# The state space of a two-layer decoder trunk: its rotation tables, its Toeplitz table and the order of its narrow products

## The chip, the core and the metric

The kernel runs on one core of a Trainium2 chip. The core has five engines with a queue each: TensorE (PE; its weight loads are shown as PEld), VectorE (DVE), ScalarE (ACT), GpSimd (POOL) and SyncE (SP, which here only issues DMAs). ACT and POOL issue DMAs too. The metric is the device time of one execution in microseconds, lower is better. All arithmetic is float32 or float32r (a float32 product whose operand is rounded; a weight is split into a high and a low part and three products make one exact one).

## What is computed

The trunk has two layers. The first is a diagonal complex state space (S5) with a gate, the second an attention layer with three branches; the change touches the first alone.

```python
u, z = split(x @ w_in, 2)                  # x: 512 x 2048, u and z: 512 x 1024
dt = exp(log_dt); mag = exp(lam_re * dt)
a = mag * exp(i * lam_im * dt)             # 64 groups x 64 states, complex
bbar = ((a - 1) / lam) * (b_re + i b_im)   # per group: 64 states x 16 channels
h[t] = a * h[t-1] + bbar @ u[t]            # per group, over 512 steps
y = real(c @ h) + d * u
g = gelu(y)
y = g * sigmoid(g @ w_glu + b_glu)
x1 = layer_norm(alpha * x + (y * silu(z)) @ w_out)
```

The kernel works the recurrence out by 64 chunks of 8 steps (`L = 8`, `NCH = 64`). Within a chunk it is a product with a Toeplitz table of the impulse response. Between chunks the states are turned by exp(-i phi chunk), which leaves a real scan. Eight tiles (`ct`) of 8 groups (`GP = 8`) are worked on one after the other.

## The kernel before

Layer 0 (`layer0_in`) multiplies x by w_in in dense products: one call of `mm3` is three products of 128x512, and 64 such calls make the first four tiles of u while x comes in, 192 more make the other twelve tiles of u and z (`L0_TILES`). Then two tiles of `g @ w_glu` follow, with two calls for each of eight k; their k-th pair needs the state space's tile k (`while s5.done < k: bg.step()`). After every call of `mm3` the scheduler `Background` is asked (`bg.tick`) to emit a stage of another chain. One such call is called a slot below. The order in which instructions are emitted is the order in which each engine works them off.

Lane 0 of the scheduler is `S5.chain`. It first runs `params` (19 stages on DVE, 4 slots apart), then the letters of `START`, then those of `CYCLE` once for each tile; a letter takes a slot. Letter t is the next stage of `tables(ct + 1)`, p of `tables(ct + 2)`, a of `apply(ct)`, r is `rotation`, and a dot is a pause. Lane 1 (`bring`) loads u of a tile back in another layout. Lane 2 holds `turns`, which `params` starts at its twelfth stage, and later `land`, which brings gelu(y) back through DRAM (`y_d`).

- `S5.__init__`, L333 to L337: POOL loads the mask `tri`; DVE zeroes a tile of tag `ta`, and POOL writes it to the front pad of the table's scratch in DRAM, `k_d`. `params` then takes the same tag `ta` for its scratch (L351), and its loads L360 to L362 (lam_re, lam_im, log_dt) wait for that write.
- `turns`, L439 to L465, on POOL: doublings of the angle, kept on the unit circle, into `AC` and `AS` (six rotations, by 8, 16, ... 256 steps). Its scratch is in tag `ta` too, so the first `tables(0)` on DVE (L513, tag `ta`) waits for its last use (L461).
- `rotation(ct)`, L467 to L491, on POOL: the tables `C` and `Sn` (128 x 8 x 64) by six doublings, 34 instructions a tile. `apply` multiplies by them at L613 (C) and L619 (Sn) and again at L629 and L631.
- `tables(ct)`, L493 to L569: DVE makes B1, B2 (L513 to L518), W1 (L528 to L533) and Q (L539, L541, L550). PE makes kps in 16 narrow instructions (L547), ACT copies it, DVE adds d, and SP writes it to `k_d` (L553). SP reads it back in one overlapping DMA as the Toeplitz table `Tz` (L558, 128 x 8 x 128), and POOL multiplies it by the mask (L560). PE transposes Q (L566), ACT copies the result to `Bst`.
- `apply(ct)`, L591 to L643, in four stages: s (L607, 16 instructions), its copy `e2` (L611), which ACT's queue sends through two DMAs that swap its halves, and L613; then L619, L620, the scan L625, another swap on SP's queue and L629; then L631 and L632 make `e1`; then the 32 instructions of yps (L636 with `Tz`, L637 with `W1` and `e1`), gelu on ACT (L640) and the DMA out.
- `SLOT`, `TPACE`, `START` and `CYCLE` are at L680 to L688.

PE runs what it is given in order, so a narrow product whose operand is late holds up the dense ones behind it.

Of the kernel before, what the change touches and what calls it, by code (L numbers as in the profile page):

```python
# [25 lines left out]
G = 64  # L26
GP = 8
L = 8
# [9 lines left out]
class Weights:  # L38
    """Streams units of 128 x <=1024 float32 from DRAM and splits each into w = h + l, both float32r."""
# [19 lines left out]
    def _split(self):  # L59
# [3 lines left out]
        if i in self.side:  # L63
            # high and low side by side, per k
# [18 lines left out]
    def ahead(self, i, loads=RAW - 1):  # L83
        """Units up to i are split, and the loads behind them are under way."""
# [13 lines left out]
class Background:  # L98
    """Stages of independent chains, put between the matrix products that they don't depend on.

    A stage yields how many products must come between it and the next of its chain, or False if it has to wait.
    """
# [55 lines left out]
def emit(tc, A, out):  # L158
# [10 lines left out]
    # the first in halves: it is waited for  # L169
# [47 lines left out]
class Core:  # L217
    """What every part uses: engines, weights, the identity."""
# [6 lines left out]
    def mm3(self, o, sh, sl, mh, ml, start, stop):  # L225
        """o (+)= s' m for s = sh + sl and m = mh + ml; what is left out, sl' ml, is below float32's rounding."""
# [10 lines left out]
def horner(V, out, x, c):  # L237
    """out = sum c[k] x**(k+1)"""
# [5 lines left out]
def exp_f32(V, x, n, r, p, ni, out):  # L244
    """out = exp(x), to float32's rounding, zero below the normal range. n, r, p, ni: scratch."""
# [16 lines left out]
def pi_parts():  # L262
    """pi cut into parts of 10 bits, so that k * part is exact for |k| < 2**14."""
# [14 lines left out]
def sincos_f32(V, th, k, r, s, t, u, sin_o, cos_o):  # L278
    """sin and cos of th: reduced by multiples of pi, Taylor series on [-pi/2, pi/2]."""
# [32 lines left out]
class S5:  # L312
    """Diagonal complex state space, by chunks of L steps.

    Rows (re | im, state) of a group; t = chunk * L + s. Within a chunk a Toeplitz product,
    between chunks a scan of the states turned by exp(-i phi chunk), which leaves it real.
    """

    def __init__(self, c, sc, gT, bg):
# [10 lines left out]
        self.AC = None  # L330
# [17 lines left out]
    def params(self):  # L348
# [61 lines left out]
        # powers of a  # L410
# [20 lines left out]
        # |a|^L  # L431
# [7 lines left out]
    def turns(self, cs, sn, c, u0, u1, u2, u3, d, e):  # L439
        """Unit rotations by 2^j theta, j = 3..8, kept on the unit circle. c, u0..3, d, e: scratch."""  # L440
        P, p1 = self.nc.gpsimd, self.p1
        AC = p1.tile([128, 6, G], F32, name="AC")
        AS = p1.tile([128, 6, G], F32, name="AS")
        c0, s0 = cs, sn
        for j in range(1, 9):
            dc, ds_ = (AC[:, j - 3], AS[:, j - 3]) if j >= 3 else ((u0, u1) if j == 1 else (u2, u3))
# [16 lines left out]
        P.tensor_scalar(AS, AS, self.sg, None, OP.mult)  # L463
        self.AC, self.AS = AC, AS
        yield 1  # L465

    def rotation(self, ct):  # L467
        P, tb = self.nc.gpsimd, self.tb
        gs = slice(ct * GP, ct * GP + GP)
        C, Sn = (tb.tile([128, GP, NCH], F32, tag=n, name=n, bufs=2) for n in ("C", "Sn"))  # L470
        t1 = tb.tile([128, GP, 32], F32, tag="rt1", name="rt1")
        t2 = tb.tile([128, GP, 32], F32, tag="rt2", name="rt2")
        P.memset(C[:, :, 0:1], 1.0)
        P.memset(Sn[:, :, 0:1], 0.0)
        for m in range(6):
            n = 1 << m
            ac = self.AC[:, m, gs].unsqueeze(2)
            as_ = self.AS[:, m, gs].unsqueeze(2)
            if n == 1:
                P.tensor_copy(C[:, :, 1:2], ac)  # L480
                P.tensor_copy(Sn[:, :, 1:2], as_)
                continue
# [1117 lines left out]
```

## Time and profile before

| | us |
|---|---|
| runs of the kernel | 1836.64, 1838.2, 1845.82 |
| median | 1838.2 |
| span of the profiled execution | 1841.3 |
| busy in it: PE, DVE, ACT, POOL | 1766.8, 1015.3, 588.4, 357.3 |

The page gives the profiled execution by its span alone; it lies between the middle and the highest of the three runs. A row of the timeline has the start, the time taken, the engine, the line, the operation, out<-in, and in brackets how long the engine had been idle before it and what released it. Matmul rows overlap (they are pipelined), so the pace is read from start to start.

### The profile page before, as it was taken

How to read it: one execution, taken by the hardware profiler on the slowest of the kernel's cores; microseconds unless marked ns; L12 is line 12 of the kernel's file. 1: busy time of each engine (PE TensorE's matmuls, PEld its weight loads, DVE VectorE, ACT ScalarE, POOL GpSimd, SP SyncE). 2: the span in 40 equal slices, each digit the busy share in tenths (PEclk: the TensorE clock that was granted, in tenths of full speed). 3: DMA queues.
4: the chain of work that ended last, by engine and by line, in shares of the span. 5: the costliest groups of instructions: out<-in, count | busy, mean ns of one | idle time of the engine just before them, and what ended most of it. 6: DMA issues, size and time to landing. Idle time of an engine off the chain costs nothing.

```text
span 1841.3 us, 22051 instructions
## 1 busy us (share of the span) xinstructions
PE 1766.8 (96%) x8455; PEld 1470.6 (80%) x8455; DVE 1015.3 (55%) x1764; ACT 588.4 (32%) x995; POOL 357.3 (19%) x500
## 2 busy tenths in 40 slices
PE   8797999999899999999999999999999999999996
PEld 6676787787778888888888888888888888888884
DVE  7775775746633355563456653555553555665336
ACT  3232232522423333332333332333332333333221
POOL 4998992002400000000000000000000000010004
PEclk9987888999999999999999999999999999999998
DMA  6443554453333322222222222222222222236332
GB/s 212 141 117 102 138 147 121 145 197 134 133 107 126 113 90 75 82 74 96 87 70 85 86 86 83 95 75 80 80 85 87 98 75 81 83 139 225 115 126 97
DMA packets 88185, 201.94 MB, mean 110 GB/s; under 512 B 24560, under 2 KB 34016, under 8 KB 87056
## 3 DMA queue, kind: packets, MB, share of 16 engines
q1 hardware_dynamic: 81392, 183.40, 29.6%
q0 software_dynamic: 3104, 10.85, 1.7%
q10 hardware_dynamic: 3584, 6.29, 1.2%
q8 instruction: 66, 1.08, 0.2%
q14 instruction: 39, 0.32, 0.1%
HBM read 176.89 MB, written 19.43 MB: 107 GB/s over the span
## 4 chain that ended last, share of the span: by engine, by line
PE 80%; POOL 9%; DVE 7%; issue 2%; DMA 2%; ACT 1%; DVEq 0%; SPq 0%; ACTq 0%; POOLq 0%
PE ps L228 23%; PE ps L230 23%; PE ps L229 22%; PE tp L1403 2%; DVE v L916 1%; POOL C L487 1%; PE s L230 1%; PE s L228 1%; PE s L229 1%; PE o L229 1%; POOL Sn L490 1%; PE o L230 1%; PE o L228 1%; POOL rt L489 1%; POOL rt L485 1%
## 5 line engine op out<-in xcount | busy, mean ns | idle before, releaser
L228 PE MATMUL ps<-x1h,hl 128*128 128x512 f32 (+1 forms) x1440 | 563.6, 391 | 1.6 <-ACT hl L77 1.6
L230 PE MATMUL ps<-x1h,hl 128*128 128x512 f32 (+1 forms) x1440 | 556.6, 387 | 0.5 <-DVE hl L79 0.5
L229 PE MATMUL ps<-x1l,hl 128*128 128x512 f32 (+1 forms) x1440 | 555.6, 386 | 0.0
L79 DVE TENSOR_TENSOR hl<-wr,hl 128x1024 fp32r<-128x1024 f32 (+1 forms) x269 | 332.1, 1238 | 319.0 <-ACT hl L77 315.3
L77 ACT CAST hl<-wr 128x1024 fp32r<-128x1024 f32 (+1 forms) x273 | 284.4, 1045 | 235.3 <-PE ps L230 206.5
L230 PEld LDWEIGHTS ps<-x1h,hl 128*128 128x128 f32 x1440 | 270.6, 188 | 57.2 <-DVE hl L79 1.0
L228 PEld LDWEIGHTS ps<-x1h,hl 128*128 128x128 f32 x1440 | 271.0, 188 | 48.2 <-ACT hl L77 1.8
L229 PEld LDWEIGHTS ps<-x1l,hl 128*128 128x128 f32 x1440 | 271.1, 188 | 46.4
L1276 POOL TENSOR_TENSOR y<-y,z 128x512 f32<-128x512 f32 x32 | 41.5, 1296 | 999.9 <-DVE z L1275 863.1
L1340 ACT ACTIVATE p<-s,m 128x384 f32<-128x384 f32 (+3 forms) x128 | 67.7, 529 | 357.5 <-DVE m L1339 357.5
L234 DVE TENSOR_TENSOR pl<-tp,ph 128x512 fp32r<-128x512 f32 (+3 forms) x128 | 62.0, 488 | 109.9 <-ACT ph L233 109.6
L228 PE MATMUL ps<-xh,hl 128*128 128x512 f32 x256 | 108.8, 425 | 6.0 <-ACT xh L751 6.0
L229 PE MATMUL ps<-xl,hl 128*128 128x512 f32 x256 | 105.3, 411 | 2.2 <-DVE xl L752 2.2
L230 PE MATMUL ps<-xh,hl 128*128 128x512 f32 x256 | 104.9, 410 | 0.8 <-DVE hl L79 0.8
L233 ACT CAST ph<-tp 128x512 fp32r<-128x512 f32 (+3 forms) x128 | 54.2, 427 | 151.3 <-PE tp L1403 151.0
L228 PE MATMUL ps<-hl,y1h 128*128 128x512 f32 x256 | 99.6, 389 | 0.0
L230 PE MATMUL ps<-hl,y1l 128*128 128x512 f32 x256 | 99.6, 389 | 0.0
L229 PE MATMUL ps<-hl,y1h 128*128 128x512 f32 x256 | 99.6, 389 | 0.0
L228 PEld LDWEIGHTS ps<-xh,hl 128*128 128x128 f32 x256 | 51.6, 202 | 17.4 <-ACT xh L751 6.0
L1339 DVE TENSOR_REDUCE m<-s 128x1 f32<-128x384 f32 (+3 forms) x128 | 62.9, 491 | 4.4
L1262 DVE SCALAR_TENSOR_TENSOR z<-z,ps 128x512 f32<-128x512 f32 x48 | 33.0, 688 | 57.1 <-ACT z L1261 57.1
L935 POOL TENSOR_TENSOR v<-v,gb 128x512 f32<-128x512 f32 x11 | 17.3, 1577 | 237.1 <-ACT v L934 237.1
(323 smaller groups left out, 2522.7 us busy)
## 6 DMA issues: line engine op xcount, KB each, us to landing
wr<-b_w_in SPq DMA_DIRECT2D x128, 512.0 KB, 3.2
wr<-kv_w SPq DMA_DIRECT2D x48, 512.0 KB, 3.2
wr<-b_w_out SPq DMA_DIRECT2D x32, 512.0 KB, 3.2
wr<-w_in_b SPq DMA_DIRECT2D x24, 512.0 KB, 3.5
wr<-w_out SPq DMA_DIRECT2D x16, 512.0 KB, 3.6
xr<-xT SPq DMA_DIRECT2D x16, 256.0 KB, 4.3
Tz<-k_d SPq DMA_DIRECT2D x8, 512.0 KB, 3.8
wr<-w_glu SPq DMA_DIRECT2D x8, 512.0 KB, 3.4
```

The lines of the kernel that those rows point to most:

```text
L77: self.nc.scalar.copy(h[:, :n], r[:, :n])
L79: eng.tensor_tensor(l[:, :n], r[:, :n], h[:, :n].bitcast(F32), OP.subtract)
L228: PE.matmul(o, sh, mh, start=start, stop=False)
L229: PE.matmul(o, sh, ml, start=False, stop=False)
L230: PE.matmul(o, sl, mh, start=False, stop=stop)
L233: self.nc.scalar.copy(h, src)
L234: self.nc.vector.tensor_tensor(l, src, h.bitcast(F32), OP.subtract)
L1262: self.nc.vector.scalar_tensor_tensor(z, z, 1.0, ps, OP.add, OP.mult)
L1276: P.tensor_tensor(y[0], y[0], z, OP.add)
L1339: self.nc.vector.tensor_reduce(m[:, b - 1, i:i + 1], s, AX.X, OP.max, negate=True)
L1340: self.nc.scalar.activation(self.p[h, b][i], s, AF.Exp, bias=m[:, b - 1, i:i + 1], accum_out=self.sums[h, b][:, i:i + 1])
L1403: PE.transpose(tp[:, 128 * (i - j):128 * (i - j) + 128], p[i][:, at:at + 128], ident)
```

## The change

- `turns` writes its six rotations into one table `R` (cos and sin, by 8, 16, 32 steps and by 64, 128, 256), with a stride of 8 elements, and then fills the other entries of two small tables of 8 with two rounds of six POOL instructions. `TPACE` is 2, not 4.
- `rotation` is six POOL instructions: products of the two small tables, broadcast along one axis each.
- `k_d` has a pad of its own for each of the 16 channels. The pad is zeroed by a memset on POOL and one DMA of 1024 runs of 448 bytes (64 before). `Tz` is read with the zeros in place, in eight DMAs, and the mask, its load and its product are gone.
- kps, s and yps are cut into 2, 2 and 4 stages, so that slots of dense products come between them. `START` has 28 letters (20 before), `CYCLE` 20 (19 before). The wait for free banks has its own letter, b, and ten pauses follow it. The rotation stands at the end of a cycle.
- gelu's output takes the buffer of `H`. The tiles of x come through seven buffers, not six.

```diff
 class S5: __init__
-        self.tri = self.p1.tile([128, L], F32, name="tri")
-        self.nc.gpsimd.dma_start(self.tri, self.A["tri"])
-        self.k_d = c.dram.tile([8, GP, PAD + 16 * 128], F32, name="k_d")
+        self.k_d = c.dram.tile([8, GP, 16, PAD + 128], F32, name="k_d")
         zero = self.tb.tile([64, PAD], F32, tag="ta", name="zero")
-        self.nc.vector.memset(zero, 0.0)
-        self.nc.gpsimd.dma_start(self.k_d[:, :, :PAD].rearrange("t g n -> (t g) n"), zero)
+        self.nc.gpsimd.memset(zero, 0.0)
+        self.nc.gpsimd.dma_start(self.k_d[:, :, :, :PAD].rearrange("t g c n -> (t g) c n"),
+                                 zero.unsqueeze(1).to_broadcast([64, 16, PAD]))
...
     def turns(self, cs, sn, c, u0, u1, u2, u3, d, e):
-        AC = p1.tile([128, 6, G], F32, name="AC")
-        AS = p1.tile([128, 6, G], F32, name="AS")
+        R = p1.tile([128, 2, 2, G, 8], F32, name="R")
+        self.R = R
+        P.memset(R[:, 0, :, :, 0], 1.0)
+        P.memset(R[:, 1, :, :, 0], 0.0)
...
+            h, at = divmod(j - 3, 3)
+            dc, ds_ = (R[:, 0, h, :, 1 << at], R[:, 1, h, :, 1 << at]) if j >= 3 else \
+                ((u0, u1) if j == 1 else (u2, u3))
...
-        P.tensor_scalar(AS, AS, self.sg, None, OP.mult)
-        self.AC, self.AS = AC, AS
+        tmp = self.tb.tile([128, 2, G, 3], F32, tag="rt1", name="rtmp")
+        for n in (2, 4):
+            sh = [128, 2, G, n - 1]
+            C, Sn = (R[:, i, :, :, 1:n] for i in range(2))
+            Co, So = (R[:, i, :, :, n + 1:2 * n] for i in range(2))
+            cn, sn_ = (R[:, i, :, :, n:n + 1].to_broadcast(sh) for i in range(2))
+            t = tmp[:, :, :, :n - 1]
+            P.tensor_tensor(Co, C, cn, OP.mult)
+            P.tensor_tensor(t, Sn, sn_, OP.mult)
+            P.tensor_tensor(Co, Co, t, OP.subtract)
+            P.tensor_tensor(So, Sn, cn, OP.mult)
+            P.tensor_tensor(t, C, sn_, OP.mult)
+            P.tensor_tensor(So, So, t, OP.add)
+            yield TPACE
+        P.tensor_scalar(R[:, 1], R[:, 1], self.sg, None, OP.mult)
+        self.turned = True
...
     def rotation(self, ct):
-        P.memset(C[:, :, 0:1], 1.0)
-        P.memset(Sn[:, :, 0:1], 0.0)
-        for m in range(6):
...
+        t = tb.tile([128, GP, NCH], F32, tag="rt1", name="rt1")
+        sh = [128, GP, 8, 8]
+        (cb, ca), (sb, sa) = ((self.R[:, i, 0, gs].unsqueeze(2).to_broadcast(sh),
+                               self.R[:, i, 1, gs].unsqueeze(3).to_broadcast(sh)) for i in range(2))
+        Cv, Sv, tv = (z.rearrange("p g (a b) -> p g a b", a=8) for z in (C, Sn, t))
+        P.tensor_tensor(Cv, ca, cb, OP.mult)
+        P.tensor_tensor(tv, sa, sb, OP.mult)
+        P.tensor_tensor(C, C, t, OP.subtract)
+        P.tensor_tensor(Sv, sa, cb, OP.mult)
+        P.tensor_tensor(tv, ca, sb, OP.mult)
+        P.tensor_tensor(Sn, Sn, t, OP.add)
...
     def tables(self, ct):
             PE.matmul(kps[:, g * 128:g * 128 + 128], B1[:, g], W1[:, g, 0:8], start=True, stop=True)
+            if g == 3:
+                yield
...
-        SP.dma_start(self.k_d[ct, :, PAD:].rearrange("g (c n) -> c g n", n=128), kp.rearrange("p g j c -> p g (j c)"))
+        SP.dma_start(self.k_d[ct, :, :, PAD:].rearrange("g c n -> c g n"), kp.rearrange("p g j c -> p g (j c)"))
         yield
         Tz = new("Tz", [GP, L, 16], 2)
-        band = self.k_d[ct, :, 0:128].rearrange("g n -> g n").unsqueeze(0)
-        SP.dma_start(Tz.rearrange("p g t c -> p g (t c)"),
-                     bass.AP(band.tensor, band.offset, [[16, 128], [PAD + 2048, GP], [1, 128]]))
-        P.tensor_tensor(Tz, Tz, self.tri.unsqueeze(1).unsqueeze(3).to_broadcast([128, GP, L, 16]), OP.mult)
+        n = PAD + 128
+        for g in range(GP):
+            band = self.k_d[ct, g, 0, 0:128].unsqueeze(0)
+            SP.dma_start(Tz[:, g].rearrange("p t c -> p (t c)"),
+                         bass.AP(band.tensor, band.offset, [[n, 16], [16, L], [1, 128]]))
...
     def apply(self, ct):
             PE.matmul(s1[:, g], t["Bst"][:, g], U[:, g], start=True, stop=True)
+            if g == 3:
+                yield
...
             PE.matmul(ys[:, g], t["W1"][:, g, 1:9].rearrange("p t c -> p (t c)"), e1[:, g], start=False, stop=True)
+            if g % 2 and g < 7:
+                yield
         self.summed = ct
-        gy = tb.tile([128, GP, NCH], F32, tag="gy", name="gy")
+        gy = tb.tile([128, GP, NCH], F32, tag="H", name="gy")
...
     def chain(self):
             elif what == "t":
-                while n == 6 and not self.banks:
+                next(t)
+            elif what == "b":
+                while not self.banks:
                     yield False
-                next(t)
-                n += 1
...
-TPACE = 4
+TPACE = 2
...
-START = 'tttttr.t.tttpp.tpr.p'
-CYCLE = 'att.ttarattp.p.pp.a'
+START = 'ttttttrb..........tttttppprp'
+CYCLE = 'aattattttatppapaaapr'
...
-    spare = ("xr", "U", "U", "e1", "e2", "H")
+    spare = ("z", "z", "U", "U", "e1", "e2", "H")
...
-            pool = st if i == 0 else s5.tb
+            pool = st if i < 2 else s5.tb
```

## Rows read from the trace of the kernel before

**Rows 1.** Stretch with the state space: busy us (instructions) by engine, clock, DMA.
```profile
71.60:333.10 261.50, 228.85 (x1135) 194.18 (x1134) 177.87 (x224) 76.52 (x110) 200.94 (x304) 0.85 0.44 125
```
**Rows 2.** Waits of PE in that stretch: us in total, times, longest us.
```profile
PE yps L636 <- POOL Tz L560: 14.8, 3, 9.6
PE kps L547 <- DVE W L533: 8.8, 1, 8.8
PE yps L637 <- DVE e L632: 5.5, 4, 2.2
```
**Rows 3.** Timeline, PE: first and last of 60 dense products, nothing between them waiting.
```profile
23.77 0.39 PE L228 MATMUL ps<-xh,hl 128*128 128x512 f32 x1
...
37.14 0.39 PE L230 MATMUL ps<-xh,hl 128*128 128x512 f32 x1
```
**Rows 4.** Timeline, PE: narrow products of one tile; of yps the first and last rows.
```profile
180.54 0.43 PE L637 MATMUL yps<-e,W 128*128 128x64 f32 x2 [0.58 <-DVE e L632]
...
183.72 0.39 PE L637 MATMUL yps<-e,W 128*128 128x64 f32 x2
185.38 1.89 PE L607 MATMUL s<-U,Bst 128*128 128x64 f32 x16
190.03 1.92 PE L547 MATMUL kps<-W,B 128*16 128x128 f32 x16
196.10 1.03 PE L566 MATMUL qps<-ident,ta 128*128 128x128 f32 x8
```
**Rows 5.** Timeline, PE: yps of another tile, where the pace changes.
```profile
262.40 0.43 PE L636 MATMUL yps<-U,Tz 128*128 128x64 f32 x2 [1.00 <-POOL Tz L560]
...
264.50 0.64 PE L637 MATMUL yps<-e,W 128*128 128x64 f32 x2
```
**Rows 6.** Timeline, POOL: the mask's product, a tile of 1024 columns.
```profile
148.51 1.93 POOL L560 TENSOR_TENSOR Tz<-Tz,tri 128x1024 f32<-128x1024 f32 x1
```
**Rows 7.** Timeline, DVE: first table W, and two operations of one state chain.
```profile
74.37 0.29 DVE L513 TENSOR_TENSOR ta<-raw,cr 128x128 f32<-128x128 f32 x1 [7.93 <-POOL AS L461]
...
78.99 1.36 DVE L533 TENSOR_TENSOR W<-ta,tb 128x1152 f32<-128x1152 f32 x1
...
134.49 1.22 DVE L625 TENSOR_TENSOR_SCAN H<-M,e 128x512 f32<-128x512 f32 x1
...
138.71 0.68 DVE L631 TENSOR_TENSOR e<-sw,Sn 128x504 f32<-128x504 f32 x1 [2.27 <-DMA sw<-H]
```
**Rows 8.** Timeline, ACT: the copy of s that its swap waits for.
```profile
163.59 0.59 ACT L611 COPY e<-s 128x512 f32<-128x512 f32 x1 [3.54 <-PE s L607]
```
**Rows 9.** DMA issues by line: queue, count, KB each, median us from issue to landing.
```profile
u_d<-gT ACTq DMA_DIRECT2D x8, 256.0 KB, 2.7
U<-u_d SPq DMA_DIRECT2D x8, 256.0 KB, 4.5
sw<-e ACTq DMA_DIRECT2D x16, 128.0 KB, 3.8
ys_d<-gy ACTq DMA_DIRECT2D x8, 256.0 KB, 2.3
gT<-ys_d SPq DMA_DIRECT2D x8, 256.0 KB, 4.8
```
**Rows 10.** Timeline, the last tile on its way to the gate: gelu, then the split.
```profile
319.71 0.60 ACT L640 ACTIVATE gy<-yps 128x512 f32<-128x512 f32 x1 [6.87 <-PE yps L637]
...
329.34 1.12 ACT L233 CAST gh<-gT 128x512 fp32r<-128x512 f32 x1 [1.54 <-DMA gT<-ys_d]
```
**Rows 11.** Timeline, SP: the issue of one read of the Toeplitz table.
```profile
204.16 0.38 SPq L558 DMA_DIRECT2D Tz<-k_d  x1
```
**Rows 12.** Timeline, the first microseconds: POOL's fill and the load behind it, then DVE.
```profile
2.24 0.58 POOL L337 DMA_DIRECT2D k_d<-zero  x1
6.72 0.52 POOL L360 DMA_DIRECT2D scratch<-lam_re  x1 [3.90 <-DMA k_d<-zero]
...
13.90 0.20 DVE L246 TENSOR_SCALAR scratch<-scratch 128x64 f32<-128x64 f32 x1 [2.46 <-DMA scratch<-log_dt]
```

More of the change, by code (lines that the diff above doesn't have):

```diff
@@ L329, in __init__ @@
         self.summed = self.done = -1
-        self.AC = None
+        self.turned = False
         self.banks = False
-        self.tri = self.p1.tile([128, L], F32, name="tri")
-        self.nc.gpsimd.dma_start(self.tri, self.A["tri"])
-        self.k_d = c.dram.tile([8, GP, PAD + 16 * 128], F32, name="k_d")
+        self.k_d = c.dram.tile([8, GP, 16, PAD + 128], F32, name="k_d")
         zero = self.tb.tile([64, PAD], F32, tag="ta", name="zero")
-        self.nc.vector.memset(zero, 0.0)
-        self.nc.gpsimd.dma_start(self.k_d[:, :, :PAD].rearrange("t g n -> (t g) n"), zero)
+        self.nc.gpsimd.memset(zero, 0.0)
+        self.nc.gpsimd.dma_start(self.k_d[:, :, :, :PAD].rearrange("t g c n -> (t g) c n"),
+                                 zero.unsqueeze(1).to_broadcast([64, 16, PAD]))
     def load(self, ct):
@@ L441, in turns @@
         P, p1 = self.nc.gpsimd, self.p1
-        AC = p1.tile([128, 6, G], F32, name="AC")
-        AS = p1.tile([128, 6, G], F32, name="AS")
+        R = p1.tile([128, 2, 2, G, 8], F32, name="R")
+        self.R = R
+        P.memset(R[:, 0, :, :, 0], 1.0)
+        P.memset(R[:, 1, :, :, 0], 0.0)
         c0, s0 = cs, sn
         for j in range(1, 9):
-            dc, ds_ = (AC[:, j - 3], AS[:, j - 3]) if j >= 3 else ((u0, u1) if j == 1 else (u2, u3))
+            h, at = divmod(j - 3, 3)
+            dc, ds_ = (R[:, 0, h, :, 1 << at], R[:, 1, h, :, 1 << at]) if j >= 3 else \
+                ((u0, u1) if j == 1 else (u2, u3))
             P.tensor_tensor(c, c0, s0, OP.subtract)
@@ L470, in rotation @@
         C, Sn = (tb.tile([128, GP, NCH], F32, tag=n, name=n, bufs=2) for n in ("C", "Sn"))
-        t1 = tb.tile([128, GP, 32], F32, tag="rt1", name="rt1")
-        t2 = tb.tile([128, GP, 32], F32, tag="rt2", name="rt2")
-        P.memset(C[:, :, 0:1], 1.0)
-        P.memset(Sn[:, :, 0:1], 0.0)
-        for m in range(6):
[L476 to L482, printed above, removed]
-            ac, as_ = ac.to_broadcast([128, GP, n]), as_.to_broadcast([128, GP, n])
-            a, b = t1[:, :, :n], t2[:, :, :n]
-            P.tensor_tensor(a, C[:, :, :n], ac, OP.mult)
-            P.tensor_tensor(b, Sn[:, :, :n], as_, OP.mult)
-            P.tensor_tensor(C[:, :, n:2 * n], a, b, OP.subtract)
-            P.tensor_tensor(a, C[:, :, :n], as_, OP.mult)
-            P.tensor_tensor(b, Sn[:, :, :n], ac, OP.mult)
-            P.tensor_tensor(Sn[:, :, n:2 * n], a, b, OP.add)
+        t = tb.tile([128, GP, NCH], F32, tag="rt1", name="rt1")
[9 more added lines that the diff above has]
+        P.tensor_tensor(Sn, Sn, t, OP.add)
         self.rot[ct] = C, Sn
@@ L648, in chain @@
         t, p = self.tables(0), self.tables(1)
-        n = 0
         for what in START:
             if what == "r":
-                while self.AC is None:
+                while not self.turned:
                     yield False
@@ L1558, in layout @@
         "w_in_b": tiles_by_column(np.concatenate([a_w_in[0][:, 512:E], a_w_in[0][:, E + by_channel]], 1)),
-        "tri": np.array([[float(t + p % L >= L - 1) for t in range(L)] for p in range(128)], np.float32),
         "lam_re": a_lam_re[0].T,
```

## The prediction

> **What bounds the kernel now.** The page gives TensorE (PE) as busy nearly throughout, and POOL as busy only in the first sixth. So the second view is the table of stretches, for the stretch from PE's first narrow product to the end of the first two gate tiles [rows 1]. Two things are to be seen there: PE was busy for 228.85 of 261.5 us, so it stood idle for 32.7 us, and its mean granted clock was 0.85. POOL was busy for 200.94 us. Third, the waits of PE name the idle time [rows 2]: 14.8 us for POOL's mask product, 8.8 us in one piece for the first W table, 5.5 us for the state `e1`. Last, the timeline gives what the work needs when nothing waits. Sixty dense products start 13.37 us from first to last, so one is 13.37 / 59 = 0.2266 us and a slot of three 0.68 us [rows 3]. A tile's narrow products at full clock are yps 3.6, s 1.9, kps 1.9 and qps 1.0, together 8.4 us [rows 4].
>
> Counting the scheduler's slots in the code, the first kps is emitted behind slot 86 of 256, and 16 slots of the gate follow: 186 x 0.68 = 126.4 us of dense work in the stretch. With 8 x 8.4 = 67.4 us of narrow work PE needs 193.8 us. The other 67.7 us are lost: 32.7 us idle and 35.0 us to the clock (PE runs at 1.2 instead of 2.4 GHz for a part). The fall can be read within one yps that had waited for 1.0 us: its pairs start by taking 0.39 us each and 2.1 us later take 0.64 [rows 5]. These 67.7 us, 3.7% of the time, are all that the change can win, since PE's products stay the same in number and size.
>
> **The change part by part.** All sums are made on the span of 1841.3 us, 3.1 us above the median of 1838.2; the difference is then taken from the median.
>
> *Mask and rotations.* POOL loses 28 of 34 instructions a tile and the mask, which takes 1.93 us for 1024 columns [rows 6]. Six products of 512 columns at half of that are about 6 us a tile where POOL now spends some 20 to 25 (200.94 over eight tiles, less the first turns). That is off the path: C is asked for a whole cycle later. What is won is PE's wait for the mask, 14.8 us [rows 2], since `Tz` comes straight from its DMA a cycle ahead, and DVE's wait for the loads of b and c, which stand behind POOL's work. The rotation moves to the end of a cycle, behind those loads on POOL's queue, so they go first; it waits for the reads of C two tiles back, which are done. Eight reads of `Tz` for one cost SP 7 x 0.38 = 2.7 us a tile [rows 11]; weight loads, u and `land` queue behind them, but are asked for five or more slots ahead. I take nothing; if that cover were gone, 2.7 us a tile.
>
> *The first tables.* `tables(0)` waits for the last use of the turns' scratch [rows 7], and this stays. W ends at 78.99 + 1.36 = 80.35 us. PE came to kps at 71.6; with the longer `START` kps is behind slot 95, nine slots later, at 71.6 + 6.1 = 77.7. Its wait falls from 8.8 to 2.6 us. The turns now write with a stride of 8 elements. No POOL row shows the price; on their 76 instructions I bound it by nothing and by 4 us and take 1.5, near the lower end because they are short. The two added rounds lie behind the last use of the scratch, so only the first rotation waits for them (C(0) is due some 10 us later). The first pieces: 4.1 us lost (2.6 to 6.6).
>
> *The zero fill.* POOL's first load of parameters waits for the fill [rows 12], DVE then for log_dt, and DVE has little room before slot 64. The fill grows from 64 to 1024 runs; the mask's load in front of it goes (0.7 us). The nearest rows are two DMAs of 256 KB [rows 9]: 2.7 us in 128 long runs, 4.5 us in 1024 short ones, so +1.8 us for the runs. That is SP's and ACT's queue; POOL builds its descriptors in software, so I take +2.0 (between -0.5, if only the mask's load counts, and +6). All of it shifts the stage, as DVE feeds PE there.
> The runs are 448 bytes. The Trainium skill (DMA: Bandwidth & Descriptors, Specifications) says that below 512 bytes a DMA reads, modifies and writes, which speaks against this fill; no row here isolates it. If it doubled the 1.8 us, the sum would be 1.8 us higher.
>
> *The pieces.* A cycle has 21 slots after, by my count, against 20, and in one the order is s, Q, the state chain, kps, transposes, yps. From the end of s to the transposes PE has 9 slots and kps: 6.1 + 1.9 = 8.0 us. They need DVE's last step of Q, which stands behind the state chain on DVE: copy of s 0.6 [rows 8], one issue 0.4, the swap 3.8 [rows 9], then two products, the scan, a product (0.7 + 0.7 + 1.2 + 0.7) and the step itself (1.2), the sizes by [rows 7]: 9.3 us. So PE waits 1.3 us, and with half a weight split (1.2 us) in between about 2.0. The wait is new, dense products queue behind it, seven cycles have it: 14 us (3 if the swap lands early and no split intervenes, 28 if it takes a microsecond more and a split always does). `e1` comes 3.0 us after the scan (135.71 to 138.71, [rows 7]) and 1.4 us of DVE: 11.8 us after s, when PE, which left the transposes late, is at yps at 9.3 + 1.0 + 2.0 = 12.3. No second wait.
>
> *The clock.* Now 35.0 us are lost, 4.3 a tile. With pieces of 0.9 us and dense slots between them the densest narrow stretch is half dense, where before yps and s stood almost back to back. I take 1.5 us a tile, 12 us. The bounds are 3 (nothing but the first wait) and 35 (no change).
>
> *The tail.* This is the part that costs. The chain ended one slot before the last dense tile; its last yps was behind slot 254 and `land` was done six slots ahead of the gate's last pair. Now it has 28 + 8 x 21 slots behind slot 77, so the last yps and `land` are all forced out in front of the gate's last pair, with nothing dense between. PE then idles through gelu 0.6 [rows 10], the store 2.3, an issue 0.4, the load 4.8 [rows 9], ACT's split 1.1 [rows 10] and about the same on DVE: 10.3 us, and 2 us at the low clock behind it: 12.3 (9 to 14).
>
> The seven tiles of x, the shared buffer of H (its next scan is eight slots behind gelu), the b and the moved memset cost nothing that a row shows.
>
> The sum of losses after: fill 2.0, first kps 4.1, gaps 14, clock 12, tail 12.3, together 44.4 us, where 67.7 are lost before. The gain is 23.3 us: 1818.0 against the span, **1815 us** against the median.
>
> **The rivals.** *The clock stays full.* If only waits bring the clock down, its term is 3 us and the time 1806; without the gaps too, 1795. For it: a yps that had hardly waited ran at full clock [rows 4]. Against: the fall in [rows 5] came with PE busy, 2 us behind a short wait.
> This is what the Trainium skill would make of it (TensorE: Matmul & The Clock Gate, Part 1): the gate follows how busy PE is, so that narrow products, which keep it busy, need no dense ones. The rows disagree in part, hence a rival.
>
> *The pieces don't help the clock.* The density of narrow products over a whole cycle is the same; if that decides, the clock still costs 35 us and the time is 1838, no change.
>
> *The state chain sets the pace (slower).* Its place is the transposes: if the swap takes the 4.8 us of `gT` [rows 9] and a whole split lies before it, each cycle waits 3.6 us, 25 in all, and waits in every cycle also bring the clock down in every cycle, some 45 us. Then 2.0 + 4.1 + 25 + 45 + 12.3 = 88 are lost, 21 more than before: 1859. It decides from a loss of (67.7 - 18.4) / 7 = 7.0 us a cycle, gap and clock together; the forecast has 3.7.
>
> **How the numbers follow.** A measurement of this kernel can tell about 0.5% from no change, 9.2 us, so faster is below 1829 and slower above 1847.4. Forecast (1806 to 1829) 0.47; full clock 0.20; no help for the clock (1829 to 1847) 0.23; slower 0.10. Faster is 0.67, same 0.23, slower 0.10. The range leaves out half of the slowest case's side and the best end: 1795 to 1842.
>
> **What would show it.** In the profile after: no wait of PE for the mask, and POOL's busy time in this stretch below half; PE's wait for the first W near 2.6 us; seven waits of about 2 us at the transposes, for DVE's Q; a clock of 0.93 or so over the stretch; a gap of about 10 us in front of the gate's last pair, behind the last yps. POOL's first load would start at about 8 us instead of 6.72. The prediction is wrong if the clock stays at 0.85, if the gaps at the transposes are twice as long, if yps waits for `e1` in most cycles, or if the gap at the tail isn't there.

## The result and the profile after

| | median, us | runs | ratio to before (95%) |
|---|---|---|---|
| before | 1839.3 | 1836.6 to 1845.8 | |
| after | 1855.4 | 1855.0 to 1858.1 | 1.0084 (1.0065 to 1.0104) |

The changed kernel is slower by 16 us (0.84%), where 23 us less were forecast; the time lies above the range. Its profiled execution has a span of 1853.9 us, 12.6 more than before. From the end of the first two gate tiles both programs need another 1508.2 us (1841.3 - 333.1 and 1853.9 - 345.7), so all of the difference of the two profiled executions arises ahead of that point. The stretch that answers to [rows 1] starts where PE comes to the first kps, at 88.02 - 7.95 = 80.07. Busy us by engine, the granted clock, DMA share and GB/s of that stretch in the kernel after:

```profile
80.07:345.70 265.63, 216.50 (x1111) 175.72 (x1112) 205.50 (x224) 77.29 (x112) 102.41 (x72) 0.88 0.44 123
```

PE's waits in the same kernel (us in total, times, longest us), which answer to [rows 2]:

```profile
PE qps L581 <- DVE ta L564: 24.3, 8, 3.8
PE kps L559 <- DVE W L545: 12.1, 2, 8.0
PE ps L228 <- ACT gh L233: 6.8, 1, 6.8
PE ps L228 <- DVE z L731: 5.4, 1, 5.4
PE yps L654 <- DVE e L649: 0.4, 1, 0.4
```

The wait for the mask [rows 2] is gone, and so nearly is the one for `e1`. In their place PE waits at all eight transposes, twice for W and twice in the gate. By the prediction's count PE needs nine slots less in this stretch, 193.8 - 6.1 = 187.7 us, so 265.6 - 187.7 = 77.9 us are lost: 49.1 idle (265.63 - 216.50) and 28.8 of busy time beyond that need, which the prediction's count puts down to the clock. Before it was 32.7 and 35.0. The same stretch in three parts (the opening, the seven cycles with their transposes, the gate) shows where the granted clock was low:

```profile
80.07:124.90 44.83, 27.46 (x116) 19.56 (x116) 42.85 (x37) 12.24 (x18) 40.70 (x28) 0.77 0.35 102
124.90:316.00 191.10, 169.32 (x914) 140.22 (x914) 149.87 (x172) 58.55 (x85) 61.70 (x44) 0.93 0.49 135
316.00:345.70 29.70, 19.72 (x81) 15.94 (x82) 12.78 (x17) 6.51 (x10) 0.00 (x0) 0.71 0.28 80
```

With PE's start 2.4 us later (80.07 against the expected place of 77.7), 77.9 - 67.7 + 2.4 = 12.6 us is the whole difference of the spans.

**The first tables** (timeline after, DVE and POOL, then PE). They answer to [rows 7]:

```profile
78.42 0.50 DVE L525 TENSOR_TENSOR ta<-raw,cr 128x128 f32<-128x128 f32 x1 [9.22 <-POOL R L467]
...
83.02 3.73 POOL L477 TENSOR_TENSOR rtmp<-R 128x384 f32<-128x384 f32 x1
...
85.77 2.19 DVE L545 TENSOR_TENSOR W<-ta,tb 128x1152 f32<-128x1152 f32 x1
...
88.02 1.89 PE L559 MATMUL kps<-W,B 128*16 128x128 f32 x8 [7.95 <-DVE W L545]
...
94.95 3.69 POOL L483 TENSOR_SCALAR R<-R,sg 128x1024 f32<-128x1024 f32 x1
98.59 0.63 POOL L343 DMA_DIRECT2D raw<-bc  x1
```

From 78.33 to 98.6 POOL fills the small tables and multiplies by the sign, and meanwhile the same DVE instructions take longer: the first product 0.50 us (0.29 before), W 2.19 (1.36). The load of the second tile's input comes only behind all this.

**One cycle** (timeline after, ACT left out):

```profile
172.59 1.22 DVE L553 TENSOR_TENSOR tb<-Y,B2s 128x1024 f32<-128x1024 f32 x1
175.33 0.69 DVE L636 TENSOR_TENSOR e<-sw,Sn 128x512 f32<-128x512 f32 x1 [1.51 <-DMA sw<-e]
...
178.70 1.22 DVE L79 TENSOR_TENSOR hl<-wr,hl 128x1024 fp32r<-128x1024 f32 x1
178.87 1.98 POOL L497 TENSOR_TENSOR C<-R 128x512 f32<-128x512 f32 x1 [11.38 <-DVE e L646]
179.84 2.09 DVE L564 TENSOR_TENSOR ta<-ta,tb 128x1024 f32<-128x1024 f32 x1
...
182.07 1.94 PE L581 MATMUL qps<-ident,ta 128*128 128x128 f32 x8 [3.32 <-DVE ta L564]
...
184.69 1.51 POOL L500 TENSOR_TENSOR Sn<-R 128x512 f32<-128x512 f32 x1
185.19 1.15 DVE L525 TENSOR_TENSOR ta<-raw,cr 128x128 f32<-128x128 f32 x1
186.16 1.12 POOL L501 TENSOR_TENSOR rt<-R 128x512 f32<-128x512 f32 x1
```

The last step of Q (L564) could have run at 173.8, but stands behind the swap, the state chain and here also a split of weights (L79) on DVE. The rotation starts as soon as L646 gives up the buffer of C, and here it lies beside that very step. The transposes then take 1.94 us, where they took 1.03 [rows 4]: the clock has fallen. The step beside the rotation isn't the rule, as its eight executions show (ns of one: least, median, most):

```profile
L564 DVE TENSOR_TENSOR ta<-ta,tb x8: 1212/1219/2090, 97.9 to 293.4; 128x1024 f32<-128x1024 f32 x8
```

It takes 2.09 us in two cycles, in which a split stands just ahead of it, and 1.21 or 1.22 in the other six, in which it starts before the rotation.

**The tail** (timeline after), answering to [rows 10]:

```profile
318.95 0.79 PE L228 MATMUL ps<-g,hl 128*128 128x512 f32 x1 [5.35 <-DVE z L731]
319.54 0.63 PE L229 MATMUL ps<-g,hl 128*128 128x512 f32 x1
...
334.45 0.60 ACT L659 ACTIVATE gy<-yps 128x512 f32<-128x512 f32 x1 [15.07 <-PE yps L654]
...
340.06 1.05 ACT L233 CAST gh<-gT 128x512 fp32r<-128x512 f32 x1 [5.02 <-DMA gT<-ys_d]
...
341.17 0.80 PE L228 MATMUL ps<-gh,hl 128*128 128x512 f32 x1 [6.75 <-ACT gh L233]
```

Besides the gap ahead of the gate's last pair, a product of the gate waits for z, which stands behind the last state chain on DVE. Behind both waits the dense products take 0.63 us.

### The profile page after: what moved, and what is told of

It is laid out like the page before. It is cut to its first block, busy times and chain, and to the rows that moved or that the text cites. A ratio compares the mean times of both kernels' runs of the same rounds, so it can differ in the third digit from the quotient of the medians.

```text
span 1853.9 us, 21889 instructions
## 1 busy us (share of the span) xinstructions
PE 1764.4 (95%) x8455; PEld 1460.6 (79%) x8455; DVE 1045.3 (56%) x1763; ACT 588.5 (32%) x995; POOL 266.3 (14%) x282
## 4 chain that ended last, share of the span: by engine, by line
PE 84%; DVE 7%; POOL 3%; DMA 2%; issue 2%; ACT 1%; ACTq 0%; DVEq 0%; POOLq 0%; SPq 0%
PE ps L228 24%; PE ps L230 23%; PE ps L229 23%; PE tp L1422 2%; DVE v L935 1%; PE s L230 1%; PE s L228 1%; PE s L229 1%; PE o L229 1%; PE o L230 1%; PE o L228 1%; PE yps L654 1%; PE cps L1187 1%; PE yps L653 1%; DMA sw<-e 1%
## 5 line engine op out<-in xcount | busy, mean ns | idle before, releaser
L79 DVE TENSOR_TENSOR hl<-wr,hl 128x1024 fp32r<-128x1024 f32 (+1 forms) x269 | 332.4, 1239 | 331.9 <-ACT hl L77 328.2
L1359 ACT ACTIVATE p<-s,m 128x384 f32<-128x384 f32 (+3 forms) x128 | 67.7, 529 | 358.1 <-DVE m L1358 358.1
L228 PE MATMUL ps<-xh,hl 128*128 128x512 f32 x256 | 113.0, 441 | 5.6 <-ACT xh L770 5.6
L230 PE MATMUL ps<-xh,hl 128*128 128x512 f32 x256 | 104.8, 409 | 2.8 <-DVE hl L79 2.8
L228 PEld LDWEIGHTS ps<-xh,hl 128*128 128x128 f32 x256 | 52.2, 204 | 17.9 <-ACT xh L770 5.6
L230 PEld LDWEIGHTS ps<-xh,hl 128*128 128x128 f32 x256 | 51.3, 200 | 15.2 <-DVE hl L79 3.2
```

Of the source, the lines that this page charges most:

```text
L79: eng.tensor_tensor(l[:, :n], r[:, :n], h[:, :n].bitcast(F32), OP.subtract)
L228: PE.matmul(o, sh, mh, start=start, stop=False)
L230: PE.matmul(o, sl, mh, start=False, stop=stop)
L1359: self.nc.scalar.activation(self.p[h, b][i], s, AF.Exp, bias=m[:, b - 1, i:i + 1], accum_out=self.sums[h, b][:, i:i + 1])
```

## The experiments

A kernel's time is its median. Each was timed beside the kernel before on its own chip, whose medians there were 1838.9 to 1841.7; the ratio with its interval is to that.

### The three parts, alone and in pairs

Rotations alone (`turns`, `rotation`, `TPACE`, and the tile buffers that make room):

```diff
-        AC = p1.tile([128, 6, G], F32, name="AC")
-        AS = p1.tile([128, 6, G], F32, name="AS")
+        R = p1.tile([128, 2, 2, G, 8], F32, name="R")
```


> Only the rotation tables as products of two small ones (with the tile buffers that make room for them); order, mask and Toeplitz transfer as before. Theory 1 (GpSimd's new strided and broadcast instructions and VectorE slow each other down where the first tables and the states are waited for): slower than before by 5 to 12 us, the first impulse product late by 3 us or more, and VectorE's short instructions above their times in the kernel before. Theory 2 (the new order of the stages is what costs): within 4 us of before, or faster by what the shorter rotations give back.

Padded table alone:

```diff
-        self.k_d = c.dram.tile([8, GP, PAD + 16 * 128], F32, name="k_d")
+        self.k_d = c.dram.tile([8, GP, 16, PAD + 128], F32, name="k_d")
-        P.tensor_tensor(Tz, Tz, self.tri.unsqueeze(1).unsqueeze(3).to_broadcast([128, GP, L, 16]), OP.mult)
```


> Only the zero-padded Toeplitz table, eight transfers and no mask; order and rotations as before. Both theories: the transfer of the zeros makes the first tables about 2 us later, and the mask's wait before the wide products ends, so faster than before by 4 to 10 us (1829 to 1835). If the wait only passes from the mask to the state chain, within 3 us of before.

Pieces and the new order alone:

```diff
-CYCLE = 'att.ttarattp.p.pp.a'
+CYCLE = 'aattattttatppapaaapr'
```


> Only the pieces and the new order of the stages; the old rotations and the mask stay. Theory 2 (order): the gap at the transposes (2 to 4 us in each of seven cycles, with a slow clock behind it) and the uncovered last tile are there, so 1850 to 1860, like the changed kernel. Theory 1 (GpSimd beside VectorE): the gaps are under 2 us each and it takes no longer than before, up to 1842.

The changed kernel without the new rotations, without the padded table, and without pieces and order (the three edits above, taken back one at a time):

```diff
-        R = p1.tile([128, 2, 2, G, 8], F32, name="R")
+        AC = p1.tile([128, 6, G], F32, name="AC")
```


> The changed kernel with the rotations of before. Theory 1: the loss is gone, at most 1840 and under the changed kernel by 15 us or more. Theory 2: within 6 us of the changed kernel, 1849 to 1858.

```diff
+        P.tensor_tensor(Tz, Tz, self.tri.unsqueeze(1).unsqueeze(3).to_broadcast([128, GP, L, 16]), OP.mult)
```


> The changed kernel with the mask and the one transfer of before: new rotations, pieces and new order. Rotations alone gave nothing and the pieces with their order cost 4.7 us. If the new rotations lose their gain under the new order and keep their price at the first tables, 1850 to 1858; if the loss of the changed kernel needs all three parts, at most 1846.

```diff
-CYCLE = 'aattattttatppapaaapr'
+CYCLE = 'att.ttarattp.p.pp.a'
```


> The changed kernel with the order of before and without pieces: new rotations and padded table. If the gains of the two parts add (-1 and -7 us), 1828 to 1832. If both end the same wait, the mask's, so that the second brings only its price (the zeros' transfer, 2 us), 1835 to 1841.

| | order of before, products whole | pieces and new order |
|---|---|---|
| old rotations, mask | 1838.9 (before) | 1843.7 (1.0032, 1.0022 to 1.0042) |
| old rotations, padded table | 1831.6 (0.9962, 0.9948 to 0.9976) | 1840.6 (1.0012, 0.9998 to 1.0026) |
| new rotations, mask | 1837.6 (0.9992, 0.9974 to 1.0009) | 1853.0 (1.0066, 1.0049 to 1.0084) |
| new rotations, padded table | 1828.7 (0.9934, 0.9917 to 0.9951) | 1855.4 (after) |

In the order of before the gains of table and rotations add up (10 us together, within the forecast): the padded table brings 7 to 9 us and the new rotations 1 to 3, which alone isn't clear of the noise. Under the new order they don't: the table does little either way (3 won, 2 lost), and the rotations cost 9 and 15. The pieces with their order cost 5 us on the old tables, 9 and 15 with one of the new ones and 27 with both. So the theory of GpSimd beside VectorE missed the rotations alone (no loss, though the first kps starts 5.8 us later, 86.2 against 80.4: DVE's waits for its inputs behind POOL fall from 26.4 to 7.1 us), and it was nearly right under the new order, where the loss goes with the rotations (1840.6, at most 1840 expected). For pieces and order alone neither theory was right: the time is low (1843.7), but the gaps are there. PE's waits in that kernel say why the first two gain nothing there:

```profile
PE qps L568 <- DVE ta L552: 27.8, 8, 4.6
PE ps L228 <- ACT gh L233: 6.7, 1, 6.7
PE ps L228 <- DVE z L717: 5.3, 1, 5.3
PE kps L547 <- DVE W L533: 2.8, 1, 2.8
```

It still has the mask, and no wait for it: the new order had ended that wait by itself. Its first W wait (2.8 us, 2.6 forecast before the price of the strides), its gaps at the transposes and its tail owe nothing to the tables, and the gaps are no shorter than the 24.3 us of the changed kernel. The kernel with the rotations alone has no wait for the mask either. There PE waits for W in its place, 21.5 us where it was 8.8 [rows 2]:

```profile
PE kps L559 <- DVE W L545: 21.5, 4, 14.2
```

In the kernel with the padded table alone the waits for W grow to 28.9 us. So the end of the mask's wait brought less than its 14.8 us also in the order of before: other waits took its place.

### The place of one step of Q

```diff
-        yield
-        V.tensor_tensor(Q, Q, qb, OP.subtract)
...
         kp = tb.tile([16, GP, L, 16], F32, tag="kp", name="kp")
```
(the step now stands ahead of these lines)

> The changed kernel with one stage moved: VectorE's subtraction that makes the transposes' input stands right behind its two products, ahead of the impulse products, and so ahead of the state chain. Order theory: the eight waits at the transposes fall from 24 us to under 8, and the slow clock behind them goes, so 1825 to 1840. Rival (VectorE's work for a cycle is what is late, in any order): the waits pass to the wide products or to the next tile's states, and it stays within 5 us of 1855.

It took 1853.7 us (1.0074, 1.0049 to 1.0100): no difference. It didn't test what it was meant to, since the letter a of the state chain still stands ahead of the step. So, with that letter exchanged:

```diff
-CYCLE = 'aattattttatppapaaapr'
+CYCLE = 'aatttatttatppapaaapr'
```


> The kernel with the subtraction ahead of the impulse products, and now one letter of the cycle exchanged, so that it also stands ahead of the state chain's third stage on VectorE (in the changed kernel, and in the run before this one, it is emitted behind it). Order theory: the waits at the transposes fall from 21 to 24 us to under 8 and the clock behind them stays full: 1832 to 1846. Rival (VectorE is late in any order): within 4 us of 1854.

1861.0 us (1.0117, 1.0097 to 1.0137), slower still. PE's waits in it:

```profile
PE yps L654 <- DVE e L649: 24.7, 7, 5.3
PE kps L561 <- DVE W L545: 13.6, 2, 6.9
...
PE qps L581 <- DVE ta L556: 2.1, 2, 1.8
```

The wait leaves the transposes, as expected, but goes whole to yps, so neither forecast of the time held. It isn't the place of this step, then, but too little time between s and yps for what DVE has to do there.

### The pieces in the order of before

```diff
-CYCLE = 'aattattttatppapaaapr'
-START = 'ttttttrb..........tttttppprp'
+CYCLE = 'aatttttarattppppaaaa'
+START = 'tttttr.t.bttttpp.tpr.p'
```


> New rotations and padded table, the narrow products in pieces, but the stages in the order of before (the pauses of the old cycle become pieces). To be compared with the kernel that has the narrow products whole in that order (1828.7). If pieces keep the clock up by themselves: 1812 to 1824. If the clock falls behind waits only: 1825 to 1833. If it is the pieces, not the order, that cost in the changed kernel: 1840 or more.

1860.1 us (1.0110, 1.0086 to 1.0135), 31 more than with the products whole. PE's waits, first with pieces, then (second fence) whole:

```profile
PE yps L654 <- DVE e L649: 16.0, 7, 3.3
PE kps L559 <- DVE W L545: 12.9, 1, 12.9
PE ps L228 <- DVE z L731: 7.3, 1, 7.3
PE ps L228 <- ACT gh L233: 6.7, 1, 6.7
PE s L622 <- ACT Bst L582: 5.3, 1, 5.3
...
```

```profile
PE kps L558 <- DVE W L544: 18.8, 4, 14.2
PE s L619 <- ACT Bst L579: 11.6, 1, 11.6
PE yps L649 <- DVE e L644: 5.4, 5, 1.8
...
```

A piece takes a letter, and with it a slot. From s (its last piece) to yps (its first) it is 15 letters with pieces and 18 with whole products; in the changed kernel it is 12. The letters also make the whole chain longer, by two in the opening and one a cycle, so that the gate waits here as in the changed kernel (7.3 + 6.7 us, 0.7 with whole products). The 31 us are therefore not those of the lost cover alone. The runs under "Cover" tell the cutting from the lost cover.

### The first tables

The rounds made tile by tile in `rotation`, the sign put into the first doubling; on the changed kernel, then on the order of before with whole products:

```diff
-            C, Sn = (R[:, i, :, :, 1:n] for i in range(2))
+            C, Sn = (self.R[:, i, :, gs, 1:n] for i in range(2))
...
-        P.tensor_scalar(R[:, 1], R[:, 1], self.sg, None, OP.mult)
+                P.tensor_scalar(ds_, e, 2.0, self.sg, OP.mult, OP.mult)
```


> The changed kernel with the two rounds that fill the small rotation tables made tile by tile inside each rotation (128x48 values in place of 128x384), and the sign put into the first of the doublings. Theory of GpSimd beside VectorE: the first tables no longer meet the long GpSimd instructions, the wait before the first impulse products falls from 8 to 3 us, the second one (4 us) goes, so 1841 to 1848. Rival (the first tables are late for another reason, as the doublings alone): within 3 us of 1855.

> New rotations and padded table in the order of before, narrow products whole, and the rounds made tile by tile with the sign put in early. To be compared with 1828.7. Theory of GpSimd beside VectorE at the first tables: the waits of 14.2 us (first impulse products) and 11.6 us (first states) fall to 5 and 3, so 1808 to 1820. Rival (what is won at the first tables is lost again at the next thing that is late): 1823 to 1831.

1847.9 us (1.0040, 1.0026 to 1.0054), 7.5 under the changed kernel, and 1819.5 (0.9893, 0.9866 to 0.9920), 9.3 under its own base. In the first the two waits for W (12.1 us) become one of 4.7, while the gaps at the transposes grow from 24.3 to 27.2; in the second the waits of 14.2 and 11.6 us become 10.6 and 2.9. Both times lie at the upper end of what was expected, and the first waits fell less than expected (to 3 and to 5 us). The second kernel is faster than the kernel before and the changed one.

### Cover

On that kernel (1819.5), three pauses moved from ahead of yps to behind it:

```diff
-CYCLE = 'att.ttarattp.p.pp.a'
+CYCLE = 'att.ttarattppppa...'
```


> The fastest kernel so far (new rotations with rounds tile by tile, padded table, narrow products whole, order of before: 1819.5) with three pauses of the cycle moved from ahead of the wide products to behind them. The length of the cycle and all products stay; between the states' products and the wide products lie 15 stages in place of 18, as in the kernel that cuts the products up in this order (there it was 1860.1 against 1828.7). Theory of the cover (the pieces cost because they take the place of dense products that covered the state chain): the waits at the wide products rise from 6 to 16 us or more and the time by 12 to 25 us, 1831 to 1845. Rival (cutting the products itself costs): within 5 us of 1819.5.

1842.0 us (1.0017, 1.0004 to 1.0030): 22.6 us for three pauses, with every product whole. PE's waits, first as it was, then with the pauses moved:

```profile
PE kps L559 <- DVE W L545: 19.6, 4, 10.6
PE yps L650 <- DVE e L645: 6.3, 6, 1.8
...
```

```profile
PE yps L650 <- DVE e L645: 17.6, 8, 4.0
PE kps L559 <- DVE W L545: 10.5, 1, 10.5
...
```

The line of half of the wide products in the same two kernels (ns of one: least, median, most; first and last start):

```profile
L650 PE MATMUL yps<-e,W x128: 275/275/422, 118.3 to 294.1; 128*128 128x64 f32 x128
```

```profile
L650 PE MATMUL yps<-e,W x128: 275/421/472, 118.7 to 312.9; 128*128 128x64 f32 x128
```

With the small ones PE's waits in all are nearly the same (thirteen each, 30.0 and 32.3 us), but the eight waits ahead of yps bring the clock down within it: the median of its products goes from 275 to 421 ns. From 71 to 350 us the mean granted clock is 0.95 and 0.88, by which I estimate 0.07 x 279 = 20 of the 22.6 us. The waits ahead of yps are also longer (2.2 us on the mean, 1.05 before); whether their place or their length decides is not shown.

And on the kernel with Q's step moved (1861.0), yps whole, without the yields between its pieces, at the place of its last piece:

```diff
-CYCLE = 'aatttatttatppapaaapr'
+CYCLE = 'aatttatttatpp.p..apr'
```


> The kernel with the subtraction ahead of the state chain (1861.0), its wide products whole again, at the place of their last piece; the other pieces stay. Between the last states' product and the wide products lie 16 stages in place of 12. Theory of the cover: the waits at the wide products fall from 24.7 us to under 8, 1838 to 1848. Rival (VectorE or the pieces' cutting itself): the waits pass elsewhere, 1855 to 1863.

1846.5 us (1.0031, 1.0015 to 1.0046), 14.5 less; the waits at yps fall from 24.7 to 10.8 us (under 8 expected).

### The opening and the tail

```diff
-START = 'ttttttrb..........tttttppprp'
+START = 'ttttttrbtttttppprp'
```


> The changed kernel without the ten pauses in the opening order, so that the chain of the state space starts and ends some 7 us earlier among the dense products. Tail theory: the 12 us that the last tile's way costs in the gate shrink by 5 to 7, so 1846 to 1851. Rival (the first tables are late by then, and the chain waits for them instead): 1852 to 1862.

1855.7 us (1.0086, 1.0066 to 1.0106). The gate's 12.5 us (6.8 + 5.4 + 0.3) fall to 2.4, but the waits for W grow from 12.1 to 24.4 us and yps waits 6.3. The rival holds: the tail's cost only changes its place.

### How POOL delays DVE

Each instruction of a rotation in two halves, on the changed kernel:

```diff
-        sh = [128, GP, 8, 8]
+        sh = [128, GP // 2, 8, 8]
+        for lo in range(0, GP, GP // 2):
```


> The changed kernel with each of the six instructions of a rotation made as two of half the length (128x256). Theory (a VectorE instruction that meets the rotation lasts until GpSimd's running instruction ends): VectorE's 128x128 products beside a rotation, 1.15 us in the changed kernel and 0.28 alone, fall to 0.5 to 0.7 us, and the time falls by 2 to 6 us, 1849 to 1853. Rival (they share a rate, whatever the length): those products stay at 1.0 us or more, and the time within 2 us of 1855.

1849.8 us (1.0058, 1.0039 to 1.0077), 5.6 less. The timeline beside a rotation:

```profile
179.03 0.71 DVE L528 TENSOR_TENSOR ta<-raw,cr 128x128 f32<-128x128 f32 x1
179.56 0.67 POOL L504 TENSOR_TENSOR rt<-R 128x256 f32<-128x256 f32 x1
179.67 0.71 DVE L529 TENSOR_TENSOR tb<-raw,sci 128x128 f32<-128x128 f32 x1
180.31 0.73 POOL L505 TENSOR_TENSOR Sn<-Sn,rt 128x256 f32<-128x256 f32 x1
```

DVE's product takes 0.71 us beside POOL instructions of 0.67 and 0.73, as it took 1.15 beside 1.12 and 1.51, and 0.29 alone (L528 at 188.8 us of the kernel after): it lasts about as long as POOL's instruction. But the 5.6 us aren't won at the transposes, where PE now waits longer than the 24.3 us of the changed kernel:

```profile
PE qps L584 <- DVE ta L567: 26.6, 8, 5.4
```

The waits for W fall from 12.1 to 8.6 us, and the mean granted clock from 71 to 350 us is 0.91 where it was 0.88. What the shorter instructions have to do with that clock is not shown, and the intervals of the two kernels overlap slightly.

### What comes last then

On the kernel of 1819.5: the doublings' scratch in room of its own, so that `tables(0)` no longer waits for it, and the zeros in another tile; then also the second tile's input loaded by SP; then also the rotations in halves.

```diff
-        self.bg.add(2, self.turns(cs, sn, e, ld, dt, x, th, new("tf"), new("tg")))
+        own = self.tb.tile([128, 7, G], F32, tag="Tz", name="own", bufs=2)
+        self.bg.add(2, self.turns(cs, sn, *(own[:, i] for i in range(7))))
```


> The fastest kernel so far (1819.5) with two tiles given room of their own: the scratch of the doublings (before it lay in the tile that the first tables write) and the source of the zeros. Theory (the first tables wait for the doublings' scratch, 8 to 9 us, and the parameters for the zeros' transfer, 2 us): the wait of 10.6 us before the first impulse products falls under 4, so 1808 to 1815. Rival (GpSimd's doublings beside the first tables take it back, or the first rotation is what comes last): 1816 to 1822.

```diff
-        self.nc.gpsimd.dma_start(raw, self.A["bc"][ct])
+        (self.nc.sync if ct == 1 else self.nc.gpsimd).dma_start(raw, self.A["bc"][ct])
```


> The kernel with room of its own for the doublings' scratch (1818.7), with the load of the second tile's input issued by SyncE and not by GpSimd, where it stands behind the doublings. Theory (that load came last: VectorE waited 6.9 us for it, ScalarE stood behind VectorE, and the first states waited 6.6 us for the copy behind that on ScalarE): the wait of 6.6 us goes, 1809 to 1815. Rival (the first rotation, which ends behind the doublings, comes last instead): 1816 to 1821.

```diff
-        sh = [128, GP, 8, 8]
+        sh = [128, GP // 2, 8, 8]
```


> The same, and each instruction of a rotation in two halves. If shorter GpSimd instructions help VectorE here as in the changed kernel (5.5 us there): 2 to 6 us under the other run of this pair. If the order of before leaves room for them: within 2 us of it.

They took 1818.7 (0.9888, 0.9871 to 0.9905), 1818.6 (0.9876, 0.9846 to 0.9906) and 1823.6 (0.9901, 0.9870 to 0.9932). Nothing is won. With the scratch apart the first kps waits 2.2 us, but the first s 6.6; with the load on SP that wait goes and the first rotation comes last. Timeline of the second kernel:

```profile
97.03 1.26 POOL L500 TENSOR_TENSOR C<-C,rt 128x512 f32<-128x512 f32 x1
...
98.32 0.69 DVE L627 TENSOR_TENSOR e<-s,C 128x512 f32<-128x512 f32 x1 [7.11 <-POOL C L500]
```

The rivals hold in the first two. In the third neither forecast held (2 to 6 us less, or within 2 us): the halves bring nothing, and whether its 5 us more are theirs stays open, as the intervals overlap.

## Why the prediction was wrong, point by point

What failed is the sum of the losses: three of its terms were too small, the first tables, the gaps at the transposes and the clock, 35 us in all. So the stretch lost 77.9 us, 10 more than before, where 42.4 were forecast (44.4 with the fill, which lies ahead of it).

**"Won: PE's wait for the mask, 14.8 us"** failed as a term. The wait goes, but the pieces' order alone ends it too, and so do the rotations alone, so in this kernel it was no gain of the padded table. The gain of that table shows only in the order of before (7 to 9 us), where it comes as well when the rotations have already ended that wait; where from is not shown.

**The zero fill, +2.0 us,** was about right. POOL's first load starts at 8.01 us (6.72, [rows 12]; 8 forecast), and PE reaches the first kps 2.4 us late; in the kernel with the padded table alone kps starts 2.0 us later than before (82.4 against 80.4). From the fill's issue to the load behind it, 4.48 us became 6.20, 1.7 more, but 7.79 in that other kernel, 3.3 more.
Had the read-modify-write of the Trainium skill's rule (DMA: Bandwidth & Descriptors, Specifications) doubled the forecast's 1.8 us, it would be 3.6 more, by the prediction's estimate; these two numbers neither show that nor rule it out, and the runs were 448 bytes long before, too.

**The first tables, 4.1 us,** failed at "the two added rounds lie behind the last use of the scratch, so only the first rotation waits for them". They lie beside DVE's first tables, and there they cost. The waits are 8.0 and 4.1 us; 7.5 us of the time go when rounds and sign are made short. W ends 7.6 us later than before: DVE's first product starts 4.0 us later (78.42 against 74.37), of which fill and strides were expected to take 3.5, and from there to the end of W it takes 9.5 us where it took 6.0. The strides themselves, with `TPACE` at 2, cost 2.3 us in the kernel with the rotations alone (76.64 against 74.37), 1.5 forecast.

**"It waits for the reads of C two tiles back, which are done"** failed. POOL, relieved of most of its work, runs ahead of DVE, so six of the eight rotations start at the moment that frees their buffer (L646), and lie beside Q's last step or the work behind it. That this lengthens PE's gaps is not shown: they are 24.3 us with the new rotations and 25.6 and 27.8 in the two kernels with the old ones under the same order.

**The gaps at the transposes, 14 us,** were of the right kind and too small: 24.3. Seven are 2.2 to 3.6 us long, 20.5 in all, and an eighth, 3.8 us, stands in the opening order, where none was reckoned. In the last six cycles it is 10.7 to 12.1 us from ACT's copy of s to the end of Q's step, where 9.3 and half a split were reckoned, 9.9. The first part, to L636, takes 5.2 to 7.5 us and not 4.8: in three of the six DVE waits there for the swap, and in the other three it comes late from a split or from Q's products. From L636 on it is 4.5 us, as reckoned, in four, and 6.6 in the two in which a whole split lies before the step and the step beside POOL.

**The clock, 12 us,** came out as 28.8, the largest miss; but 28.8 is a remainder (busy time beyond the need), and the granted clock tells where the term was too small. In the seven cycles it is 0.93, some 0.07 x 191 = 13 us, so for them 12 was about right. What the term hardly held is the low clock of the opening, with the two waits for W, and of the gate (0.77 and 0.71 there, partly while PE idles). The reason given, "the densest narrow stretch is half dense", isn't shown either: the pieces of yps do run at full clock (median 275 ns), but whole they do so too in the kernels of 1828.7 and 1819.5, where they hardly wait. Waits cost more: the run with three pauses moved loses some 20 us of clock for 2 us more of idle time. The rival "the clock stays full" had this condition right, and the condition was not met.

**The tail, 12.3 us,** came out near that size (12.5 idle, the clock not counted), in part by luck. The gap that was described, ahead of the gate's last pair, is 7.1 us (6.8 + 0.3) where 10.3 were reckoned; the other 5.4 came at z, which the prediction hadn't seen.

**No second wait at yps** was right: 0.4 us, because the first wait left the transposes as late as reckoned.

**The rival that came nearest** was the state chain that sets the pace: 25 us of gaps and 1859 against 24.3 and 1855. Its point of decision, 7.0 us a cycle, was passed: (24.3 + 28.8) / 7 = 7.6. Its gaps were right in kind, as the swap is late in three cycles of six and a split in the way in others. That its time is so near is partly luck: it took 45 us for the clock, 16 too many, and 4.1 for the first tables, 8 too few. The misses of the forecast add up: first tables 8.0, gaps 10.3, clock 16.8, together 35.1 of the 77.9 - 42.4 = 35.5 us by which the stretch lost more than the forecast without its fill.

## What to carry to other kernels

Slots of dense work are cover for a chain on another engine; a cut that puts a piece into a slot takes that cover away, so count the slots between a chain's start and its consumer before and after (18 to 12 here, against some 15 us of chain). Put work with large instructions on POOL only where DVE has nothing urgent, and expect a relieved engine to run ahead, up to the instruction that frees its buffer. A wait that an edit ends is not yet time won: each of the three parts alone ends the mask's 14.8 us, and they won 1 and 7 us and lost 5. What a wait costs in the clock behind it can be far more than the wait.

## What the runs showed of the hardware

- A product of DVE and an instruction of POOL beside it take turns by whole instructions. A 128x128 product of two inputs on DVE takes 0.29 us alone, 0.71 beside POOL instructions of some 0.7 us and 1.15 beside those of 1.1; POOL's 128x384 product took 3.73 us beside DVE, where the other five of that size took 1.19 to 2.13. The Trainium skill (SBUF — State Buffer, Who interferes with whom) has the same: the pair of ports that the two share is locked for a whole instruction and the other blocks. The trace agrees, by the halves above.
- The sum and number of PE's waits don't tell what they cost in clock: thirteen waits of 30.0 us in all, 6.3 of them ahead of yps, went with a mean clock of 0.95 from 71 to 350 us; thirteen of 32.3 us, 17.6 of them ahead of yps, with 0.88.
